# Four column blocks share the opening of a two-block transformer kernel, rows turned beforehand, and sixteen modulation units change place

## The chip, the cores and the metric

The kernel runs on one core of a Trainium2 chip. The metric is the time of one execution on the device in microseconds (us). A core has a matrix engine (TensorE, PE in the rows; its weight loads are PEld), an elementwise engine (VectorE, DVE), an activation engine (ScalarE, ACT), GpSimd (POOL) and SyncE (SP), which here issues the transfers from device memory. Each engine takes its instructions strictly in the order in which they were written for it; semaphores between engines hold an instruction until its inputs are there. SBUF is the on-chip memory with 128 partitions; PSUM has eight banks that matmuls write.

## The reference

256 rows of 1024 features go through two layers of a first block and two of a second. A layer of the first block, cut to what matters here (`cond` is one vector, the same for all rows):

```python
mod = cond @ ada_w[l] + ada_b[l]
sh1, sc1, g1, sh2, sc2, g2, sh3, sc3, g3 = jnp.split(mod, 9, axis=-1)
hn = _modulate(_rms_norm(h, norm_g[l, 0]), sh1, sc1)      # xn * (1 + scale) + shift
h = h + 0.5 * g1 * _swiglu(hn, ffn1_w_in[l], ffn1_w_out[l])
hn = _modulate(_rms_norm(h, norm_g[l, 1]), sh2, sc2)
z = hn @ w_in[l]
# four groups of z: differential attention, convolution, gMLP, forgetting attention
h = h + g2 * (mixed @ w_out[l])
hn = _modulate(_rms_norm(h, norm_g[l, 2]), sh3, sc3)
h = h + 0.5 * g3 * _swiglu(hn, ffn2_w_in[l], ffn2_w_out[l])
```

All of it is float32. `ada_w` is 1024 x 9216 for each layer, so the nine modulation vectors cost 36 MB of weights a layer and next to no matrix work.

## The kernel before

The 256 rows are two row tiles (`tt`), the 1024 features eight feature tiles (`k`) of 128. A float32 product is made from three products of float32r parts: high x high, high x low, low x high. A weight **chunk** is 128 x 1024 numbers, 512 KB: for an input projection two feature tiles by the 512 columns of one column block `b`, so a block has four chunks (`c`); a feed-forward's input has 11 blocks. SyncE loads a chunk (`fetch`, L391 to L401, at most eight outstanding), ScalarE casts it to the high part, and VectorE subtracts that from the chunk to get the low part (`pump`). A stage of one chunk and one row tile is then six matmuls of 128x512.

Modulation comes in **units** of 512 KB, 128 of a vector's 1024 values: VectorE multiplies the unit by the broadcast `cond_row` and sums along the row (`ada_unit`; in the trace CUSTOM_DVE_ANT_0 with `cond_row` among its inputs). Gate vectors (v = 2, 5, 8) go another way, as a running sum with `cond`. Units and chunks lie in one `stream` in the order in which they are loaded and worked on. A table, `among` (L369), spreads the units of the vectors among the chunks of a part: a part is a feed-forward or a mixing of one layer. For the first feed-forward part of layer 0 it names vectors 2, 4, 3, 5 (32 units); for layer 0's mixing vectors 7 and 6 (16 units); the mixing of layer 1 has none.

**The opening.** At the start nothing is there: the first modulation vectors (scale 1, shift 0) and the first weights are loaded together. For c = 0 to 3 the stream holds two feature tiles of scale and shift (four units) and then chunk `c` of the first EARLY = 3 column blocks, so that TensorE can begin with the first two feature tiles. The order of its work is then chunk, row tile, block (`gemm_in`, first lines). The rows are normalized (VectorE, per row), turned by TensorE against an identity into PSUM, four feature tiles to a bank, and ScalarE reads the bank, multiplies by the scale and adds the shift (`ev<-bank,mod,mod`), casts, and VectorE makes the low part (`to_xT`, L695, in four steps of two feature tiles for the first norm). After the opening the other blocks go one after the other, each with all eight feature tiles; a block's result is read from its bank by ScalarE and VectorE (`ev<-bank`, `ev<-ev,bank`), an evacuation.

**What sets the order.** The kernel is written by a Python planner that keeps a clock for each engine (`Plan`, with a cost for each kind of operation). `pump` converts the next chunk or unit when it has landed by the planner's clock and the engines are not too late; `chunk` forces a conversion when TensorE's program needs it; `Background` interleaves the row work and the attention steps. The order that results is fixed at build time. Every recorded operation has the line of the recording helper, L183, so that rows are told apart by their tiles: `c` are buffers of the arena, `bank` PSUM banks, `mod` the modulation vectors, `ev`, `sm`, `st`, `dl` small work tiles, `con` constants.

Of the kernel before, what the change touches and what calls it, by code (L numbers as in the profile page):

```python
# [242 lines left out]
def two_blocks(ctx: ExitStack, tc, w, out, dbg=None, stages=99):  # L243
# [9 lines left out]
    EARLY = 3  # L253
# [115 lines left out]
    among = {0: (modulation(0, 2, 4, 3, 5), 2, 48), 1: (modulation(0, 7, 6), 16, 32), 2: (modulation(0, 8) + modulation(1, 1, 0, 2), 10, 60),  # L369
# [42 lines left out]
    def pump(force=False, most=None, goal=None):  # L412
        while True:
# [7 lines left out]
            if not force and plan.ready(raw) > plan.now + 0.3:  # L421
                return
# [117 lines left out]
    def ada_unit(raw, l, v, kt):  # L540
        key = (l, v)
        if v % 3 != 2:
# [28 lines left out]
    def mod_tile(l, v):  # L571
        if (l, v) not in mod_val:
            mod_val[l, v], mod_there[l, v] = pool.tile([P, KT], F, name=f"mod{l}_{v}"), []
# [21 lines left out]
    class Normed:  # L595
# [3 lines left out]
        def __init__(self, mods=None, gain=None, keep=False, steps=2):  # L599
            self.mods, self.gain, self.keep, self.steps = mods, gain, keep, steps  # L600
# [35 lines left out]
        def chain(self, tt):  # L636
# [9 lines left out]
            by = (lambda pair: all(pair in mod_there.get(m, ()) for m in self.mods), lambda: [mod_val[m] for m in self.mods]) if self.mods else None  # L646
# [4 lines left out]
            yield from to_xT(rows, self.gain, self.xT[tt], by, self.x[tt], there=self.there[tt], have=lambda hf: self.halves[tt] > hf, steps=self.steps)  # L651
# [6 lines left out]
        def finish(self, tt, pair):  # L658
            wait(lambda: len(self.there[tt]) > pair * self.steps // 4, "rows")
# [35 lines left out]
    def to_xT(src, A, dst, mods=None, whole=None, there=None, have=lambda hf: True, steps=2):  # L695
# [14 lines left out]
        def modulated(step):  # L710
            return mods is None or all(mods[0](p) for p in range(4 * step // steps, 4 * (step + 1) // steps))

        yield from turn()
        B = None
        if mods:
            if steps == 2 and not modulated(0):
                yield from turn()
            yield from until(lambda: modulated(0))
            A, B = mods[1]()
        n = KT // steps  # L720
        for step in range(steps):
            hf = step * 2 // steps
            if hf == len(banks):
                yield from turn()
            yield from until(lambda: modulated(step) and (A is None or whole is not None or evr.has(1)))
            a = slice(n * step, n * step + n)
            ps = banks[hf][:, a.start - 4 * hf:a.stop - 4 * hf]
            if A is None:
                split(ps, hi[:, a], lo[:, a])
                psr.put()  # L730
                there.append(step)
                continue
            x = evr.take([P, n, P]) if whole is None else whole[:, a]
            if B is None:
                ve.tensor_tensor(x, ps, A[:, a, None].to_broadcast([P, n, P]), op=OP.mult)
            else:
                for j in range(n):
                    k = n * step + j
                    if steps == 2 and hf:
# [3 lines left out]
            if a.stop == 4 * hf + 4:  # L743
                psr.put()
            split(x, hi[:, a], lo[:, a])
            there.append(step)
            if whole is None:
                evr.put()

# [16 lines left out]
    def gemm_in(n_, blocks, evac):  # L766

        whole, nb = range(4), len(blocks)
        if st["want"] == 0:
            order = [(b, tt, whole[c:c + 1]) for c in whole for tt in range(2) for b in range(EARLY)]  # L770
            order += [(b, tt, whole) for b in range(EARLY, nb) for tt in range(2)]
            mine["quota"] = 4
        else:
            order = [(b, tt, whole) for b in range(nb) for tt in range(2)]
            if len(n_.there[1]) < 2:
# [3 lines left out]
        for b, tt, part in order:  # L779
# [6 lines left out]
            for ci in part:  # L786
# [4 lines left out]
                n_.finish(tt, ci)  # L791
                for k2 in range(2):
                    k = 2 * ci + k2
# [993 lines left out]
```

## Time and profile before

| | |
|---|---|
| median of 3 runs | 1932.78 us (1932.68 to 1933.05) |
| profiled execution, its own time | 1931.21 us |
| its span in the trace | 1929.3 us |
| mean granted clock of TensorE | 0.993 |
| TensorE busy | 1871.3 us, 97% |
| VectorE busy | 1307.2 us, 68% |
| ScalarE busy | 969.6 us, 50% |
| transfers | 397.31 MB, mean 206 GB/s |

TensorE is busy nearly all of the span, and the share of a stage is read from the windows: first the opening (22.6 us, the first float32r matmul, to 58.6), then the rest of layer 0's first feed-forward part (to about 228.6, where the mixing's 128x260 matmuls begin), layer 0's mixing (to 356.4), and layer 1's mixing (745.0 to 848.9). The granted clock of a stretch is in parts of 2.4 GHz; the engine's other level is 1.2 GHz, which a row shows as 0.50.

### The profile page before, as it was taken

How to read it: one execution, taken by the hardware profiler on the slowest of the kernel's cores; microseconds unless marked ns; L12 is line 12 of the kernel's file. 1: busy time of each engine (PE TensorE's matmuls, PEld its weight loads, DVE VectorE, ACT ScalarE, POOL GpSimd, SP SyncE). 2: the span in 40 equal slices, each digit the busy share in tenths (PEclk: the TensorE clock that was granted, in tenths of full speed). 3: DMA queues.
4: the chain of work that ended last, by engine and by line, in shares of the span. 5: the costliest groups of instructions: out<-in, count | busy, mean ns of one | idle time of the engine just before them, and what ended most of it. 6: DMA issues, size and time to landing. Idle time of an engine off the chain costs nothing.

```text
span 1929.3 us, 23834 instructions
## 1 busy us (share of the span) xinstructions
PE 1871.3 (97%) x8672; PEld 1491.6 (77%) x8672; DVE 1307.2 (68%) x2055; ACT 969.6 (50%) x1501; POOL 17.0 (1%) x56
## 2 busy tenths in 40 slices
PE   5999997999999999999999999999999999999998
PEld 3888864688888887658888787888888787888886
DVE  5988598687878876966575646666664646666562
ACT  4544534543544445464454645545553655655451
POOL 0000000000000000000000000000000000000000
PEclk9999998999999999999999999999999999999999
DMA  9988584387868885526574343654574443655460
GB/s 385 335 301 324 177 309 151 108 297 268 320 224 301 291 320 191 184 83 219 176 269 155 121 164 109 201 193 153 163 246 148 142 153 99 199 195 163 144 228 33
DMA packets 110578, 397.31 MB, mean 206 GB/s; under 512 B 12278, under 2 KB 12406, under 8 KB 110460
## 3 DMA queue, kind: packets, MB, share of 16 engines
q1 hardware_dynamic: 109020, 391.88, 58.6%
q10 hardware_dynamic: 1440, 3.91, 0.6%
q8 instruction: 68, 1.11, 0.2%
q14 instruction: 50, 0.41, 0.1%
HBM read 394.69 MB, written 1.05 MB: 205 GB/s over the span
## 4 chain that ended last, share of the span: by engine, by line
PE 85%; DVE 7%; ACT 5%; DMA 2%; issue 1%; POOLq 0%; SPq 0%; POOL 0%; DVEq 0%; ACTq 0%
PE bank L183 85%; DVE c L183 5%; ACT c L183 2%; ACT sm L183 2%; DMA c<-in_ffn_w_in_dram 2%; DVE sm L183 1%; ACT L175 1%; DVE st L183 0%; DMA c<-in_w_out_b_dram 0%; ACT ev L183 0%; DVE ev L183 0%; DMA col<-in_cols_dram 0%; DVE h L183 0%; ACT dl L183 0%; ACT st L183 0%
## 5 line engine op out<-in xcount | busy, mean ns | idle before, releaser
L183 PE MATMUL bank<-c,c 128*128 128x512 f32 (+3 forms) x7392 | 1764.4, 397 | 19.7 <-ACT c L183 15.0
L183 PEld LDWEIGHTS bank<-c,c 128*128 128x128 f32 (+1 forms) x7392 | 1352.2, 189 | 335.7 <-issue 44.7
L183 DVE TENSOR_TENSOR c<-c,c 128x1024 fp32r<-128x1024 f32 (+3 forms) x604 | 709.0, 1197 | 242.6 <-ACT c L183 234.9
L183 ACT CAST c<-c 128x1024 fp32r<-128x1024 f32 (+1 forms) x590 | 588.7, 1036 | 110.3 <-PE bank L183 79.4
L183 ACT ACTIVATE ev<-bank 128x256 f32<-128x256 f32 (+1 forms) x100 | 40.1, 401 | 202.5 <-PE bank L183 202.1
L183 DVE CUSTOM_DVE_ANT_0 c<-c,cond_row,col 128x1024 f32<-128x1024 f32 x96 | 121.9, 1279 | 0.0
L183 ACT CAST c<-bank 128x512 fp32r<-128x512 f32 (+1 forms) x100 | 55.3, 553 | 85.1 <-PE bank L183 85.1
L183 DVE TENSOR_TENSOR c<-bank,c 128x512 fp32r<-128x512 f32 (+2 forms) x108 | 69.9, 649 | 24.4 <-ACT c L183 24.1
L183 DVE TENSOR_TENSOR ev<-ev,bank 128x256 f32<-128x256 f32 x88 | 36.7, 418 | 69.2 <-ACT ev L183 67.8
L183 ACT ACTIVATE ev<-bank,st 128x512 f32<-128x512 f32 x56 | 38.5, 687 | 77.5 <-PE bank L183 77.5
L183 ACT ACTIVATE junk<-h 128x512 f32<-128x512 f32 x44 | 27.7, 631 | 98.2 <-DVE h L183 97.8
L183 PE MATMUL bank<-con,ev 128*128 128x128 f32 x432 | 72.4, 273 | 3.3 <-DVE ev L183 3.3
L183 PEld LDWEIGHTS bank<-con,ev 128*128 128x128 f32 x432 | 55.7, 139 | 25.1 <-issue 3.7
L183 ACT CAST c<-ev 128x512 fp32r<-128x512 f32 (+1 forms) x36 | 20.6, 573 | 91.6 <-DVE ev L183 91.2
L183 ACT ACTIVATE c<-bank,st 128x512 f32<-128x512 f32 x36 | 24.8, 688 | 75.2 <-PE bank L183 69.7
L183 DVE TENSOR_TENSOR ev<-bank,c 128x512 f32<-128x512 f32 x40 | 27.4, 686 | 40.8 <-PE bank L183 40.7
L183 DVE SCALAR_TENSOR_TENSOR c<-c,cond,c 128x1024 f32<-128x1024 f32 x42 | 53.8, 1280 | 0.0
L183 DVE TENSOR_TENSOR ev<-ev 128x512 f32<-128x512 f32 x32 | 22.1, 691 | 45.5 <-ACT ev L183 45.5
L183 DVE SCALAR_TENSOR_TENSOR c<-c,col,c 128x256 f32<-128x256 f32 x120 | 48.8, 479 | 0.0
L183 ACT ACTIVATE sm<-sm,st 128x128 f32<-128x128 f32 x72 | 31.8, 442 | 26.0 <-DVE st L183 26.0
L183 DVE TENSOR_TENSOR c<-ev,c 128x512 fp32r<-128x512 f32 (+1 forms) x36 | 22.8, 633 | 29.8 <-ACT c L183 29.7
L183 DVE TENSOR_TENSOR h<-h,bank 128x512 f32<-128x512 f32 x16 | 10.9, 683 | 42.1 <-PE bank L183 42.1
(104 smaller groups left out, 681.8 us busy)
## 6 DMA issues: line engine op xcount, KB each, us to landing
c<-in_ffn_w_in_dram SPq DMA_DIRECT2D x176, 512.0 KB, 5.7
c<-in_w_in_dram SPq DMA_DIRECT2D x152, 512.0 KB, 4.1
c<-in_ada_w_dram SPq DMA_DIRECT2D x144, 512.0 KB, 5.5
c<-in_ffn_w_out_dram SPq DMA_DIRECT2D x88, 512.0 KB, 5.2
c<-in_w_up_dram SPq DMA_DIRECT2D x64, 512.0 KB, 3.7
c<-in_w_down_dram SPq DMA_DIRECT2D x64, 512.0 KB, 3.8
c<-in_w_out_dram SPq DMA_DIRECT2D x16, 512.0 KB, 6.3
c<-in_w_o_dram SPq DMA_DIRECT2D x16, 512.0 KB, 4.7
```

Source lines behind the costliest of these rows:

```text
L175: self.eng.preload_act_table_set(table)
L183: return fn(*args, **kw)
```

## The change

EARLY goes from 3 to 4, so that four column blocks share the opening, and their eight banks (four blocks, two row tiles) are held at once. The order is chunk, block, row tile. For the first norm, `to_xT` gives way to `first_xT`: all sixteen 128x128 transposes come first and ScalarE copies them from PSUM to an SBUF tile `x`; scaling, cast and split then go from there, in steps that end at 1, 2, 4, 6 and 8 feature tiles (`FIRST`). The matmuls wait for a feature tile, not for a pair. The factor (1 + scale) x g is made once for all eight columns, except for the first norm, where it follows the steps. `pump` holds back unforced conversions until the opening's sixteen chunks are made, and `chunk` forces up to two. In the table `among`, vectors 7 and 6 of layer 0 move from its mixing to its first feed-forward part: 48 units at positions 0 to 50 there, none in the mixing. The main lines:

```diff
-    EARLY = 3
+    EARLY = 4
+    FIRST = [1, 2, 4, 6, 8]
...
-    among = {0: (modulation(0, 2, 4, 3, 5), 2, 48), 1: (modulation(0, 7, 6), 16, 32), 2: (modulation(0, 8) + modulation(1, 1, 0, 2), 10, 60),
+    among = {0: (modulation(0, 2, 4, 3, 5, 7, 6), 0, 50), 2: (modulation(0, 8) + modulation(1, 1, 0, 2), 10, 60),
...
-            if not force and plan.ready(raw) > plan.now + 0.3:
+            if not force and (st["made"] < 4 * EARLY or plan.ready(raw) > plan.now + 0.3):
                 return
...
-            pump(True, goal=i + 1 if i < 4 * EARLY else None)
+            pump(True, goal=min(i + 2, 4 * EARLY) if EARLY <= i < 4 * EARLY else i + 1 if i < EARLY else None)
...
-            if kt % 2:
+            if kt + 1 in (FIRST if key in ((0, 0), (0, 1)) else [KT]):
+                a = slice(mod_there[key], kt + 1)
                 if v % 3 == 1:
-                    a = slice(kt - 1, kt + 1)
-                    ve.scalar_tensor_tensor(t[:, a], t[:, a], 1.0, K("norm_g", 24 * l + 8 * (v // 3) + kt - 1, 2), op0=OP.add, op1=OP.mult)
-                mod_there[key].append(kt // 2)
+                    ve.scalar_tensor_tensor(t[:, a], t[:, a], 1.0, K("norm_g", 24 * l + 8 * (v // 3) + a.start, a.stop - a.start),
+                                            op0=OP.add, op1=OP.mult)
+                mod_there[key] = a.stop
...
+    def first_xT(src, dst, mods, there):
+
+
+        hi, lo = dst
+        yield from until(room)
+        x = arena.take([P, KT, P])
+        for hf in range(2):
+            yield from ripe(src[:, 512 * hf:512 * hf + 512])
+            yield from until(aux_free)
+            ps = aux((P, 4, P))
+            for j in range(4):
+                k = 4 * hf + j
+                pe.transpose(ps[:, j], src[:, P * k:P * k + P], ident)
+            sc_.copy(x[:, 4 * hf:4 * hf + 4], ps)
+            psr.put()
+            there.append(0)
+        for a in (slice(a, b) for a, b in zip([0] + FIRST, FIRST)):
+            made = 0 if a.stop == 1 else 1 if a.stop == 2 else EARLY * (a.start // 2) + 2
+            yield from until(lambda: mods[0](a.stop) and st["made"] >= made)
+            A, B = mods[1]()
+            for k in range(a.start, a.stop):
+                sc_.activation(x[:, k], x[:, k], AF.Identity, scale=A[:, k:k + 1], bias=B[:, k:k + 1])
+            split(x[:, a], hi[:, a], lo[:, a])
+            there.append(a.stop)
+            yield
+        arena.put()
...
-            order = [(b, tt, whole[c:c + 1]) for c in whole for tt in range(2) for b in range(EARLY)]
+            order = [(b, tt, whole[c:c + 1]) for c in whole for b in range(EARLY) for tt in range(2)]
             order += [(b, tt, whole) for b in range(EARLY, nb) for tt in range(2)]
-            mine["quota"] = 4
+            mine["quota"] = 8
...
-                n_.finish(tt, ci)
                 for k2 in range(2):
                     k = 2 * ci + k2
+                    n_.finish(tt, k)
...
-    begin(lambda: all(norms[0].rs[tt] is not None for tt in range(2)))
+    begin(lambda: all(len(norms[0].there[tt]) == 2 for tt in range(2)))
     pump(True, 4)
-    begin(lambda: all(norms[0].there))
+    begin(lambda: all(len(norms[0].there[tt]) == 3 for tt in range(2)))
```

Three places show how the order of instructions moves. The first is VectorE's queue in the second stage of the opening, before: the last modulation unit, the splits of the two row tiles (`c_139`, `c_151`), three low parts of weights (128x1024), and the next stage's first unit.

```order
L183 ISA c_133,mod_0_127<-c_133,cond_row,col 128x1024
L183 ISA mod_0_127 128x1
L183 TENSOR_TENSOR c_139<-ev_221,c_138 128x256
L183 TENSOR_TENSOR c_151<-ev_231,c_150 128x256
L183 TENSOR_TENSOR c_246<-c_136,c_245 128x1024
L183 TENSOR_TENSOR c_259<-c_167,c_258 128x1024
L183 TENSOR_TENSOR c_271<-c_176,c_270 128x1024
L183 ISA c_182,mod_1_123<-c_182,cond_row,col 128x1024
```

The same place of the changed kernel, where the row splits are `c_108` and `c_123`:

```order
L183 ISA c_167,mod_0_158<-c_167,cond_row,col 128x1024
L183 ISA mod_0_158 128x1
L183 TENSOR_TENSOR c_275<-c_180,c_274 128x1024
L183 TENSOR_TENSOR c_281<-c_206,c_280 128x1024
L183 TENSOR_TENSOR c_108<-c_109,c_107 128x256
L183 TENSOR_TENSOR c_123<-c_124,c_122 128x256
L183 TENSOR_TENSOR c_319<-c_226,c_318 128x1024
L183 TENSOR_TENSOR c_325<-c_246,c_324 128x1024
L183 ISA c_262,mod_1_153<-c_262,cond_row,col 128x1024
```

There is one low part of a weight more, and two of the four stand ahead of the row splits. The second place is VectorE's queue at the end of the opening, before: the last row splits, low parts of weights, and between them the evacuations of the opening's banks (`ev_...<-ev_...,bank_...`).

```order
L183 TENSOR_TENSOR c_139<-ev_378,c_138 128x256
L183 TENSOR_TENSOR c_151<-ev_383,c_150 128x256
L183 TENSOR_TENSOR c_401<-c_305,c_400 128x1024
L183 TENSOR_TENSOR c_416<-c_327,c_415 128x1024
L183 TENSOR_TENSOR c_425<-c_342,c_424 128x1024
L183 TENSOR_TENSOR c_431<-c_351,c_430 128x1024
L183 TENSOR_TENSOR ev_440<-ev_439,bank_162 128x256
L183 TENSOR_TENSOR c_447<-c_354,c_446 128x1024
L183 TENSOR_TENSOR ev_456<-ev_455,bank_190 128x256
```

The same place of the changed kernel. Here `c_554` and `c_560` are the low parts of the opening's chunks 14 and 15, which are the last chunks of column blocks 2 and 3; the banks 175, 194, 201 and 214 belong to blocks 0 and 1.

```order
L183 TENSOR_TENSOR ev_516<-ev_515,bank_175 128x256
L183 TENSOR_TENSOR ev_527<-ev_526,bank_194 128x256
L183 TENSOR_TENSOR ev_537<-ev_536,bank_201 128x256
L183 TENSOR_TENSOR ev_550<-ev_549,bank_214 128x256
L183 TENSOR_TENSOR c_554<-c_415,c_553 128x1024
L183 TENSOR_TENSOR c_560<-c_421,c_559 128x1024
L183 TENSOR_TENSOR c_569<-c_448,c_568 128x1024
```

Before, all of the opening's low parts stand ahead of the first evacuation; now two stand behind four evacuations. The third place is VectorE's queue within layer 0's mixing, before: units of vector 7 (`mod_7_2137`), the finishing operation of a pair, and products of the convolution (`c_2141`).

```order
L183 TENSOR_TENSOR c_2284<-c_2108,c_2283 128x1024
L183 ISA c_2110,mod_7_2137<-c_2110,cond_row,col 128x1024
L183 ISA mod_7_2137 128x1
L183 SCALAR_TENSOR_TENSOR mod_7_2137<-mod_7_2137,col 128x2
L183 ISA c_2139,mod_7_2137<-c_2139,cond_row,col 128x1024
L183 ISA mod_7_2137 128x1
L183 ISA c_2207,mod_7_2137<-c_2207,cond_row,col 128x1024
L183 ISA mod_7_2137 128x1
L183 SCALAR_TENSOR_TENSOR mod_7_2137<-mod_7_2137,col 128x2
L183 ISA c_2248,mod_7_2137<-c_2248,cond_row,col 128x1024
```

The same place of the changed kernel (`c_2167` is the convolution there):

```order
L183 TENSOR_TENSOR c_2222<-c_2001,c_2221 128x1024
L183 SCALAR_TENSOR_TENSOR c_2167<-c_2040,col,c_2167 128x256 x8
L183 TENSOR_TENSOR dl_2203<-bank_2160,st_2242 128x8x64
L183 TENSOR_REDUCE st_2257<-ev_2256 128x8
L183 TENSOR_TENSOR c_2264<-c_2092,c_2263 128x1024
L183 SCALAR_TENSOR_TENSOR c_2167<-c_2040,col,c_2167 128x256 x8
```

The units are gone from between the weights' low parts, the convolution and the attention's steps.

## Rows read from the trace of the kernel before

**Rows 1.** Windows by stage: stretch, length, busy (instructions), granted clock, DMA share, GB/s.

```profile
22.60:58.60 36.00, 32.35 (x117) 24.97 (x117) 29.24 (x44) 17.12 (x29) 0.00 (x0) 0.91 1.03 409
58.60:208.70 150.10, 150.07 (x679) 123.03 (x680) 125.29 (x164) 74.74 (x100) 0.00 (x0) 1.00 0.83 295
...
228.60:356.40 127.80, 109.34 (x455) 70.97 (x453) 103.97 (x268) 62.24 (x144) 0.97 (x5) 0.93 0.54 194
...
745.00:848.90 103.90, 100.19 (x456) 65.82 (x454) 83.61 (x231) 62.18 (x145) 0.97 (x5) 1.00 0.47 160
```

**Rows 2.** Timeline, VectorE, first stage: start, busy, operation, [idle before, releaser].

```profile
14.47 1.28 DVE L183 CUSTOM_DVE_ANT_0 c<-c,cond_row,col 128x1024 f32<-128x1024 f32 x1
...
19.49 0.08 DVE L183 DVE_READ_ACCUMULATOR2_ANT mod<- 128x1 f32 x1
20.54 0.43 DVE L183 TENSOR_TENSOR c<-ev,c 128x256 fp32r<-128x256 f32 x1 [0.96 <-ACT c L183]
21.68 0.43 DVE L183 TENSOR_TENSOR c<-ev,c 128x256 fp32r<-128x256 f32 x1 [0.72 <-ACT c L183]
22.63 3.50 DVE L183 TENSOR_TENSOR c<-c,c 128x1024 fp32r<-128x1024 f32 x3 [0.52 <-ACT c L183]
26.04 1.28 DVE L183 CUSTOM_DVE_ANT_0 c<-c,cond_row,col 128x1024 f32<-128x1024 f32 x1
```

**Rows 3.** Timeline, TensorE, the opening.

```profile
22.65 0.80 PE L183 MATMUL bank<-c,c 128*128 128x512 f32 x1 [6.92 <-ACT c L183]
23.91 7.94 PE L183 MATMUL bank<-c,c 128*128 128x512 f32 x23 [0.46 <-DVE c L183]
...
32.48 11.25 PE L183 MATMUL bank<-c,c 128*128 128x512 f32 x48
45.80 0.49 PE L183 MATMUL bank<-c,c 128*128 128x512 f32 x1 [2.07 <-ACT c L183]
47.05 11.23 PE L183 MATMUL bank<-c,c 128*128 128x512 f32 x36 [0.76 <-DVE c L183]
58.63 3.70 PE L183 MATMUL bank<-c,c 128*128 128x512 f32 x15 [0.34 <-DVE c L183]
```

**Rows 4.** Windows, TensorE alone: stretch, length, busy, granted clock, DMA share, GB/s.

```profile
46.00:54.00 8.00, 7.24 (x19) 0.57 1.03 409
760.00:768.00 8.00, 5.75 (x24) 1.00 0.23 91
```

**Rows 5.** Windows of the instructions on `cond_row`: length, VectorE, ScalarE, clock, DMA.

```profile
60.00:208.70 148.70, 20.45 (x16) 0.00 (x0) 1.00 0.83 294
228.60:356.40 127.80, 20.14 (x16) 0.00 (x0) 0.93 0.54 194
745.00:848.90 103.90, 0.00 (x0) 0.00 (x0) 1.00 0.47 160
```

**Rows 6.** Windows, all engines, the stretch of layer 0's mixing that holds its units.

```profile
248.90:304.00 55.10, 47.61 (x198) 34.41 (x197) 54.62 (x132) 17.89 (x45) 0.00 (x0) 0.93 0.81 300
```

**Rows 7.** Timeline, TensorE, layer 0's mixing.

```profile
301.62 1.65 PE L183 MATMUL bank<-c 32*128 32x256 f32 x6 [7.49 <-DVE c L183]
```

**Rows 8.** Groups by line and shape, 0 to 230: count, busy us, mean ns, idle before.

```profile
L183 DVE TENSOR_TENSOR c<-c,c 128x1024 fp32r<-128x1024 f32 x72 | 86.1, 1221 | 10.3 <-ACT c L183 9.1 <-issue 1.1
L183 ACT CAST c<-c 128x1024 fp32r<-128x1024 f32 x72 | 72.0, 1048 | 14.9 <-PE bank L183 14.8
...
L183 ACT ACTIVATE ev<-bank 128x256 f32<-128x256 f32 x22 | 8.5, 385 | 34.8 <-PE bank L183 34.6
...
L183 ACT ACTIVATE ev<-bank,mod,mod 128x128 f32<-128x128 f32 x16 | 6.9, 454 | 25.4 <-DVE mod L183 25.4
...
L183 ACT CAST ones_r<-con 128x128 fp32r<-128x128 f32 x1 | 0.3, 290 | 0.0
```

**Rows 9.** Waits, 58.6 to 208.7: who waits for whom, us in total, times, longest.

```profile
DVE ev L183 <- ACT ev L183: 7.0, 5, 1.7
DVE c L183 <- ACT c L183: 7.0, 10, 2.6
```

More of the change, by code (lines that the diff above doesn't have):

```diff
@@ L650, in chain @@
                 self.x[tt] = arena.take([P, KT, P])
-            yield from to_xT(rows, self.gain, self.xT[tt], by, self.x[tt], there=self.there[tt], have=lambda hf: self.halves[tt] > hf, steps=self.steps)
+            if self.first:
+                yield from first_xT(rows, self.xT[tt], by, self.there[tt])
+            else:
+                yield from to_xT(rows, self.gain, self.xT[tt], by, self.x[tt], there=self.there[tt], have=lambda hf: self.halves[tt] > hf)
             if self.mods:
@@ L656, in chain, with finish @@
             st["hurry"] -= 1
-        def finish(self, tt, pair):
-            wait(lambda: len(self.there[tt]) > pair * self.steps // 4, "rows")
+        def finish(self, tt, k):
+            wait(lambda: self.there[tt] and self.there[tt][-1] > k, "rows")
         def free(self):
@@ L693, in start, with to_xT @@
                 (nc.sync, nc.scalar)[hf].dma_start(out[tt * P:tt * P + P, s], h[tt][:, s])
-    def to_xT(src, A, dst, mods=None, whole=None, there=None, have=lambda hf: True, steps=2):
+    def to_xT(src, A, dst, mods=None, whole=None, there=None, have=lambda hf: True):
         hi, lo = dst
@@ L715, in to_xT @@
         if mods:
-            if steps == 2 and not modulated(0):
+            if not mods[0](KT):
                 yield from turn()
-            yield from until(lambda: modulated(0))
+            yield from until(lambda: mods[0](KT))
             A, B = mods[1]()
-        n = KT // steps
-        for step in range(steps):
-            hf = step * 2 // steps
+        for hf in range(2):
             if hf == len(banks):
                 yield from turn()
-            yield from until(lambda: modulated(step) and (A is None or whole is not None or evr.has(1)))
-            a = slice(n * step, n * step + n)
-            ps = banks[hf][:, a.start - 4 * hf:a.stop - 4 * hf]
+            yield from until(lambda: A is None or whole is not None or evr.has(1))
+            a, ps = slice(4 * hf, 4 * hf + 4), banks[hf]
             if A is None:
@@ L730, in to_xT @@
                 psr.put()
[L731 removed]
+                there.append(a.stop)
                 continue
[L733 removed]
+            x = evr.take([P, 4, P]) if whole is None else whole[:, a]
             if B is None:
[L735 removed]
+                ve.tensor_tensor(x, ps, A[:, a, None].to_broadcast([P, 4, P]), op=OP.mult)
             else:
[L737 to L739 removed]
+                for j in range(4):
+                    k = 4 * hf + j
+                    if hf:
                         ve.tensor_scalar(x[:, j], ps[:, j], A[:, k:k + 1], B[:, k:k + 1], op0=OP.mult, op1=OP.add)
@@ L1614, in two_blocks @@
         for i in range(3):
-            norms.append(Normed(mods=((l, 3 * i + 1), (l, 3 * i)), keep=i == 1, steps=2 if norms else 4))
+            norms.append(Normed(mods=((l, 3 * i + 1), (l, 3 * i)), keep=i == 1, first=not norms))
     for l in range(L):
```

21 lines of the change are left out of this document (11 added, 10 removed).

## The prediction

> **What bounds the kernel now.** I read the windows by stage first, then one engine's rows inside the stages that the edit touches. In [rows 1] TensorE is busy for 150.07 of 150.10 us in the rest of the first feed-forward part (58.6 to 208.7): there only TensorE's own work counts, and VectorE's 125.29 us and the transfers (share 0.83) are cover. Two stretches are different. In the opening, 22.6 to 58.6, TensorE has 32.35 of 36.00 at a granted clock of 0.91. In layer 0's mixing, 228.6 to 356.4, it has 109.34 of 127.80 at 0.93. Layer 1's mixing, the same computation without modulation units [rows 5], takes 103.90 with 100.19 busy at 1.00. So the two mixing parts differ by 23.9 us: TensorE idles 18.46 us in one and 3.71 in the other, which is 14.75, and the other 9.15 is time in which its work went slower.
>
> What holds the opening is a turn-taking of VectorE and ScalarE, seen in [rows 2]. VectorE reduces four modulation units (14.47 to 19.57), waits 0.96 for ScalarE's cast of the first row tile, splits it, waits 0.72 for the second, then 0.52 for the cast of a weight chunk, then makes three low parts (3.50); only then come the next four units, at 26.04. The period is 11.57 us, 2.20 of it waiting. TensorE gets 36 matmuls in a period; 48 of them took 11.25 [rows 3], so it needs 8.44 and runs dry: it stood still before 45.80 (2.07) and before the 47.05 row (0.76), and in the 8 us from 46 on its granted clock was 0.57 [rows 4], the lower of its two levels (1.2 and 2.4 GHz) for most of it, a loss of 0.43 x 8 = 3.4 us.
>
> What holds layer 0's mixing is VectorE between 248.9 and 304.0: 54.62 of 55.10 us busy [rows 6]. All 16 units lie in that stretch, 20.14 us [rows 5]. TensorE's 7.49 idle us there are one stop before 301.62, released by VectorE [rows 7]; the later stops in this part follow from that delay.
>
> **The opening.** After the change the row tiles are turned first: 16 transposes and four ScalarE copies that fall before 18 us. They cost nothing, because ScalarE's first modulation work waits for VectorE's first units anyway (two of the four are done at 17.0; the second row tile is ready at 14.5, and its two copies of 128x512, each at most two of the 128x256 reads at 0.39, take 1.5 behind the transposes [rows 2, 8]). TensorE's start then follows from the rows. First feature tile: two units end at 14.47 + 5.10/2 = 17.0; ScalarE scales and casts two tiles of 128x128, 2 x (0.45 + 0.29), and casts the first chunk, 1.05 [rows 8]: 19.6, against 22.65 before. The second matmul waits for the low part: four units end at 19.57, two small splits (0.29 each, estimated from the cast of the same shape) and a subtraction (3.50/3 = 1.17) give 21.3 plus two semaphore steps, 21.5, against 23.91.
>
> Then stages of four column blocks. VectorE per stage: four units 5.10, four subtractions 4.67, two row splits 0.86, together 10.6. ScalarE: four casts of 1.05, four scalings of 0.45, two casts at most as long as the splits, 6.9. Transfers: eight units of 524 KB at 409 GB/s [rows 1], 10.25. TensorE: 48 matmuls, 11.25. TensorE is the longest, provided that VectorE no longer waits its 2.20; the first order shows why it need not: two weight subtractions now stand between the units and the row splits, two behind them. The first 23 matmuls took 7.94 where 23 x 0.2344 = 5.39, a slow start of 2.55, which I keep. Stage 0 ends at 21.5 + 47 x 0.2344 + 2.55 = 35.1, stage 1 at 46.3, and the 110th matmul starts 13 later, at 49.4. Before it started at 58.63 [rows 3]. **Term 1: -9.2 us**; if VectorE keeps its waits the period is 12.8, 1.55 a stage for three stages, and the term is -4.5. I take -9.2, since the rows behind each wait have been moved.
>
> The Trainium skill speaks against this: "DMA: Bandwidth & Descriptors", Specifications, gives a limit of about 358 GB/s from device memory to one core, by which a stage of eight units would take 11.7 us, above TensorE's 11.25, and four stages about 1.9 us more, for a predicted time of 1910.1. The row shows 409 GB/s over 36 us; the measurement decides.
>
> **A new stop at its end.** The second order shows what the edit does behind the last stage: the subtractions of chunks 14 and 15 (inputs c_415, c_421) now stand behind the evacuations of four banks, and ScalarE's casts do likewise. The last evacuation's bank is finished only when TensorE has done column block 1's second row tile, and by then TensorE needs chunk 14. So it stands for one ScalarE activation (0.39), one cast (1.05) and one subtraction (1.22, slightly more than one of three in a row): 2.66 [rows 8]. That a half clock follows is seen behind the stop of 2.83 at 46 (3.4 lost) and not in 760 to 768, where TensorE stood for 2.25 of the 8 us and the clock stayed 1.00 [rows 4]; bounds 0 and 3.4, and I take 2.0, since the new stop's length is nearer to the first. **Term 2: +4.7**, between 2.7 and 6.1.
>
> On the clock the Trainium skill ("TensorE: Matmul & The Clock Gate", What's actually happening) says that the low level is the default and that activity lifts it, so that every stop can cost it again; by that alone the stop would be 6.1 and the time 1909.6. The row of 760 to 768 shows a pause that did not.
>
> **Sixteen units into the first feed-forward part.** They cost VectorE 20.45/16 = 1.28 each there [rows 5], 20.4. VectorE's idle time in that stretch is 150.10 - 125.29 = 24.8, so it would be at 145.7 of 150.1; the transfers would be 44.3 + 8.4 MB at 409 GB/s, 129 us. Cover is there, but thin: if it fails, the price is rival B's. SyncE issues these loads in the order of the stream, up to eight ahead, so a unit that waits for VectorE delays the weight loads behind it; weight casts and subtractions queue behind units on VectorE in the same way. **Term 3: 0**, bounds 0 and 9.3; a gain is excluded, since TensorE had 0.03 us idle there.
>
> **Layer 0's mixing.** Without its units VectorE has 34.5 us of work in a stretch of 55.1, and SyncE 16 fewer loads. The third order shows products of the attention and weight subtractions following one another directly. The nearest row above is layer 1: -23.9. The nearest below is the one stop in the full stretch: -7.5. I take the 20.1 us that leave a VectorE that is full; what is late next is TensorE itself, busy 100.19 of 103.90 in layer 1 [rows 1]. **Term 4: -20.1.**
>
> The finishing of a modulation vector in one operation for eight columns in place of four, and the waits by feature tile in place of pairs, take away a few operations on 128x2 pieces, under a busy TensorE: nothing.
>
> **Sum.** -9.2 + 4.7 + 0 - 20.1 = -24.6 on the profiled execution's 1931.21: 1906.6. That execution lies 1.57 under the median of 1932.78, so the median comes to 1908.2.
>
> **Rivals.**
> **B, VectorE becomes the bound of the first feed-forward part.** Its waits for ScalarE there were 7.0 and 7.0 us [rows 9]. If they remain, it needs 125.3 + 20.1 + 14.0 = 159.4 against 150.1: +9.3, a time of 1917.5. For it: the stretch before had cover of only 24.8 us. Against: it waits for ScalarE where its queue holds nothing else that is ready, and sixteen more units are such work. The transfers would do the same if they were slower than their row: from 22.6 on this stretch and the opening move 14.7 + 44.3 + 8.4 = 67.4 MB [rows 1], which at 409 GB/s are there at 187.4, 17 us before the stretch ends at 204.2. By the 358 GB/s of the Trainium skill ("DMA: Bandwidth & Descriptors", Specifications) they would be there at 210.8, 6.6 late, for a time of 1914.8; the row of [rows 1] with 409 speaks against it.
> **C, mixing gives back only its one stop.** The remaining idle and slow time is layer 0's own order: -7.5 for -20.1, and 1920.8. Against it speaks that layer 1 has neither.
> **D, no new stop and the whole difference of the layers:** -9.2 - 23.9 = -33.1, a time of 1899.7. It needs the casts of chunks 14 and 15 to be done earlier than their place in the queue allows.
> **E, slower.** The stop of term 2 comes back at each of the seven later column blocks of this part, since each one's subtractions can land behind the evacuation of the block before, with VectorE now 97% full: 7 x 4.7 = 32.9, which gives +8.3 and 1941.1. It decides from the sixth stop on. Against: TensorE ran through this stretch with the same queues, and only the opening holds four blocks open at once.
> **F, it does not do what it says.** VectorE keeps its turn-taking (-4.5), the stop takes that back (+4.7), and the 20.1 us come back as TensorE's waits in the stretch that takes the units: 1933.
>
> **How the numbers follow.** Forecast 0.57, B 0.18, C 0.12, D 0.06, E 0.04, F 0.03. The forecast's own bounds: best -9.2 + 2.7 - 23.9 = -30.4 (1902.4), worst of its terms -4.5 + 6.1 - 20.1 = -18.5 (1914.3). To hold 8 in 10 the range goes from D to C, 1899 to 1921; E and F stay out. Measurement can tell about 0.2%, 3.9 us, from no change: faster 0.93, same 0.03, slower 0.04.
>
> **What would show it.** First matmul at 19.6, 110th matmul at about 49.4, VectorE waiting under 1 us a stage; one stop of about 2.7 us near 63, with or without clock 0.5 behind it; the first 128x260 matmul at about 224 in place of 228.6, with TensorE over 149 busy in any 150 before it; mixing 104 to 110 us long. Wrong would be a stage period near 12.8, several stops between 66 and 205, or a mixing part that still idles 10 us.

## The result, and the profile after

The changed kernel takes 1906.26 us (median of 4 runs, 1904.18 to 1907.24) against 1932.91 for the kernel before beside it (4 runs, 1932.68 to 1934.27). The ratio is 0.9859, with a 95% interval of 0.9842 to 0.9876. The prediction was 1908.2 in a range of 1899 to 1921, faster with a chance of 0.93. The profiled execution of the changed kernel took 1907.24 us, with a span of 1905.5: 23.8 us less span than before.

Windows by stage of the changed kernel answer to [rows 1] (stretch, length; busy and instructions of TensorE, weight loads, VectorE, ScalarE and GpSimd; granted clock, DMA share, GB/s):

```profile
19.70:60.90 41.20, 40.36 (x168) 32.89 (x169) 37.28 (x74) 26.46 (x44) 0.00 (x0) 1.00 1.03 410
60.90:70.50 9.60, 7.11 (x34) 5.17 (x31) 8.19 (x10) 6.74 (x10) 0.00 (x0) 1.00 1.03 410
70.50:202.00 131.50, 130.65 (x589) 106.77 (x590) 127.25 (x160) 61.45 (x79) 0.00 (x0) 1.00 0.95 361
...
222.00:330.30 108.30, 103.64 (x452) 67.47 (x450) 84.05 (x233) 60.22 (x143) 0.74 (x2) 0.97 0.45 151
...
720.00:825.00 105.00, 101.25 (x451) 66.45 (x451) 82.97 (x229) 61.05 (x142) 0.74 (x2) 0.98 0.46 156
```

The opening is full: 40.36 of 41.20 us of TensorE, where it had 32.35 of 36.00. VectorE has 127.25 of 131.50 in the feed-forward part and TensorE still 130.65. Layer 0's mixing is 108.3 us long, not 127.8, and close to layer 1's.

The timeline of VectorE in the second stage, which answers to [rows 2] (start, busy, operation, [idle before, releaser]):

```profile
25.72 1.28 DVE L183 CUSTOM_DVE_ANT_0 c<-c,cond_row,col 128x1024 f32<-128x1024 f32 x1
...
30.74 3.03 DVE L183 TENSOR_TENSOR c<-c,c 128x1024 fp32r<-128x1024 f32 x4
33.99 2.36 DVE L183 TENSOR_TENSOR c<-c,c 128x1024 fp32r<-128x1024 f32 x2 [0.23 <-ACT c L183]
36.27 1.28 DVE L183 CUSTOM_DVE_ANT_0 c<-c,cond_row,col 128x1024 f32<-128x1024 f32 x1
```

The period is 36.27 - 25.72 = 10.55 us with four column blocks, and of the 2.20 us of waiting 0.23 is left. The row of four is two weight subtractions and two row splits without a wait between them.

TensorE's timeline up to the mixing answers to [rows 3] (only rows behind an idle time are shown):

```profile
19.78 0.80 PE L183 MATMUL bank<-c,c 128*128 128x512 f32 x1 [3.22 <-ACT c L183]
21.34 39.79 PE L183 MATMUL bank<-c,c 128*128 128x512 f32 x167 [0.76 <-DVE c L183]
...
62.75 0.49 PE L183 MATMUL bank<-c,c 128*128 128x512 f32 x1 [1.41 <-ACT c L183]
64.01 0.73 PE L183 MATMUL bank<-c,c 128*128 128x512 f32 x2 [0.77 <-DVE c L183]
...
70.81 0.44 PE L183 MATMUL bank<-con,ev 128*128 128x128 f32 x2 [0.63 <-DVE ev L183]
...
99.45 0.73 PE L183 MATMUL bank<-c,c 128*128 128x512 f32 x2 [0.55 <-DVE c L183]
```

From 21.34 on, 167 matmuls follow one another; then come the new stop (1.41 and 0.77) and two small ones.

Four points in the program, and its end, show where the time went (start of the operation in us; the last column is the difference).

| | before | after | |
|---|---|---|---|
| 110th float32r matmul of the opening | 58.63 | 47.59 | -11.04 |
| first row of 128x260 matmuls (the mixing begins) | 228.62 | 222.07 | -6.55 |
| last transposes of layer 0's mixing | 356.46 | 330.36 | -26.10 |
| last transposes of layer 1's mixing | 848.89 | 824.35 | -24.54 |
| end of the span | 1929.3 | 1905.5 | -23.8 |

(In the changed kernel three of the 128x260 matmuls, 0.12 us each, stand ahead of that row, so that the second line is 0.35 us short of the real difference, and the mixing's 108.3 is 0.35 us short of a like length.) Counted alike, the opening gives 11.0, the stops behind it take 4.1 back, the mixing gives 19.2, and 2.3 are lost where nothing was changed.

### The profile page after: what moved, and what is told of

The parts are those of the page before. It is cut to its first block, busy times and chain, and to the rows that moved or that the text cites. A ratio compares the mean times of both kernels' runs of the same rounds, so it can differ in the third digit from the quotient of the medians.

```text
span 1905.5 us, 23848 instructions
## 1 busy us (share of the span) xinstructions
PE 1864.3 (98%) x8672; PEld 1487.9 (78%) x8672; DVE 1303.6 (68%) x2044; ACT 972.5 (51%) x1506; POOL 17.0 (1%) x56
## 4 chain that ended last, share of the span: by engine, by line
PE 87%; DVE 5%; ACT 5%; issue 1%; DMA 1%; POOL 0%; ACTq 0%; POOLq 0%; DVEq 0%
PE bank L183 87%; DVE c L183 3%; ACT sm L183 2%; ACT c L183 2%; DVE sm L183 1%; ACT L175 1%; DMA cond_row<-in_c_dram 0%; DVE ev L183 0%; DMA c<-in_ada_w_dram 0%; DMA c<-in_w_out_b_dram 0%; DVE st L183 0%; DVE h L183 0%; ACT ev L183 0%; ACT junk L183 0%; ACT dl L183 0%
## 5 line engine op out<-in xcount | busy, mean ns | idle before, releaser
L183 DVE TENSOR_TENSOR c<-c,c 128x1024 fp32r<-128x1024 f32 (+4 forms) x614 | 711.5, 1182 | 233.4 <-ACT c L183 225.4
L183 ACT CAST c<-c 128x1024 fp32r<-128x1024 f32 (+4 forms) x600 | 592.0, 1025 | 112.7 <-PE bank L183 74.7
L183 ACT CAST c<-ev 128x512 fp32r<-128x512 f32 x28 | 17.4, 620 | 91.4 <-DVE ev L183 91.2
L183 DVE TENSOR_TENSOR c<-ev,c 128x512 fp32r<-128x512 f32 x28 | 19.4, 692 | 23.1 <-ACT c L183 23.0
```

What stands on the lines that cost most here:

```text
L183: return fn(*args, **kw)
```

## The experiments

The theory: the opening gains because VectorE no longer takes turns with ScalarE; the mixing gains because VectorE was full there; in the feed-forward part the units are covered. Rival B held that VectorE becomes the bound there. Each ratio below is against runs of the kernel before made beside that experiment. Their medians were 1931.14 to 1931.42 us, 1.5 to 1.8 below the 1932.91 of the result, so that a difference of a few us between an experiment and the changed kernel's 1906.26 is partly this one.

**The units alone.** The kernel before with one line of the table (the units spread over positions 0 to 54, where the changed kernel has 0 to 50):

```diff
-    among = {0: (modulation(0, 2, 4, 3, 5), 2, 48), 1: (modulation(0, 7, 6), 16, 32), 2: (modulation(0, 8) + modulation(1, 1, 0, 2), 10, 60),
+    among = {0: (modulation(0, 2, 4, 3, 5, 7, 6), 0, 54), 2: (modulation(0, 8) + modulation(1, 1, 0, 2), 10, 60),
```

> The kernel before with one line changed: vectors 7 and 6 of layer 0 move from its mixing to the first feed-forward part (positions 0 to 54 there); the opening keeps three blocks. My theory (the units cost layer 0's mixing 20 us because VectorE is full there, and are covered in the feed-forward part): the mixing takes 108 us in place of 127.8, the first 128x260 matmul stays within 2 us of 228.6, the time is 1912 to 1915. Rival B (VectorE becomes the bound where the units go): the 128x260 matmul comes 5 to 9 us later and the time is 1918 to 1922.

1917.25 us, ratio 0.9926 (0.9909 to 0.9942), above my 1912 to 1915 and just below the rival's range. The mixing did what the theory said, 106.3 us long (234.46 to 340.80). The 128x260 matmuls came at 234.46, 5.8 us later than before, as rival B had it. TensorE's timeline had two idle rows there, and ScalarE's shows what stood before them:

```profile
74.69 0.49 PE L183 MATMUL bank<-c,c 128*128 128x512 f32 x1 [2.68 <-ACT c L183]
75.95 0.73 PE L183 MATMUL bank<-c,c 128*128 128x512 f32 x2 [0.76 <-DVE c L183]
```

```profile
66.07 1.28 ACT L175 ACT_TABLE_LOAD   x1
69.42 0.20 ACT L183 ACTIVATE st<-st 128x2 f32<-128x2 f32 x1 [2.07 <-DVE st L183]
70.86 0.20 ACT L183 ACTIVATE st<-st 128x2 f32<-128x2 f32 x1 [1.23 <-DVE st L183]
...
71.27 1.28 ACT L175 ACT_TABLE_LOAD   x1
72.56 0.66 ACT L183 ACTIVATE ev<-bank 128x256 f32<-128x256 f32 x2
73.11 0.59 ACT L183 CAST c<-bank 128x512 fp32r<-128x512 f32 x1
73.57 2.96 ACT L183 CAST c<-c 128x1024 fp32r<-128x1024 f32 x3
```

From 66.07 to 72.55 ScalarE did little but the per-layer preparation: two table loads and two tiny activations that waited for VectorE. The casts of weights stood behind it. From 76 to 80 the granted clock was 0.57, another 1.7 us. So the delay could be the preparation's place, not VectorE's load; the next run parts the two.

**The units alone, with the preparation put off.** Besides the line above:

```diff
     def layer_setup(l):
+        yield from until(lambda: plan.now > 120.0)
```

> The kernel before with the sixteen units moved and, besides, the small per-layer preparation (gains, two table loads on ScalarE) put off until 120 us of the planner's clock. In the run that moved the units alone, the first 128x260 matmul came at 234.5 in place of 228.6, with one stop of 2.68 and 0.76 us at 74.7 behind that preparation, and half the clock behind it. My theory (the preparation's new place made that stop, VectorE's load did not): no stop near 75, the 128x260 matmul at 228 to 230, the time 1910 to 1913. Rival B (VectorE is the bound where the units go): stops elsewhere between 60 and 200, the 128x260 matmul still at 233 or later, 1916 or more.

1912.82 us, ratio 0.9902 (0.9887 to 0.9916), and the 128x260 matmuls at 228.86, 0.24 from where they were before. The window of the rest of the feed-forward part (columns as above):

```profile
58.60:208.70 150.10, 150.10 (x680) 122.94 (x681) 144.16 (x201) 74.85 (x100) 0.00 (x0) 1.00 0.93 351
```

VectorE has 144.16 of 150.10 us, 18.9 more than in [rows 1], and TensorE has no idle time at all. Rival B falls: the cover holds at 96%, with this spread of the units.

**The opening alone.** The changed kernel with the old table:

```diff
-    among = {0: (modulation(0, 2, 4, 3, 5, 7, 6), 0, 50), 2: (modulation(0, 8) + modulation(1, 1, 0, 2), 10, 60),
+    among = {0: (modulation(0, 2, 4, 3, 5), 2, 48), 1: (modulation(0, 7, 6), 16, 32), 2: (modulation(0, 8) + modulation(1, 1, 0, 2), 10, 60),
```

> The changed kernel with the old table: vectors 7 and 6 stay in layer 0's mixing, the opening is the new one. My theory (the two edits add up): the first 128x260 matmul at 221 to 222.5, the mixing again 126 to 129 us long, the time 1925 to 1927. Rival (the opening's gain is given back later when VectorE's load stays in the mixing, or the mixing was already part of the opening's gain): the time is 1930 or more, or 1915 or less.

1922.85 us, ratio 0.9956 (0.9942 to 0.9971): 2.15 us below my range, between my case and the rival's. The 128x260 matmuls came at 222.75, 0.25 past my range, and the mixing kept its stop:

```profile
222.70:351.80 129.10, 110.80 (x455) 71.43 (x453) 103.52 (x265) 62.42 (x144) 0.97 (x5) 0.91 0.53 192
```

```profile
295.30 1.65 PE L183 MATMUL bank<-c 32*128 32x256 f32 x6 [6.91 <-DVE c L183]
```

129.1 us, against 127.8 in [rows 1] and 108.3 with the units gone. The profiled execution of this kernel took 1926.42 us and lay above its other three (1921.94 to 1923.66), so this one profile shows the marks, and not where the others were 3 to 4 us shorter. The two edits add up: 0.44% for the opening and 0.98% for the units (with the preparation out of the way) make 1.42%, and both together measured 1.41%. Each of the three is known to some 0.15%, and the run for the units has the wider spread and the later preparation, so the sum agrees within that and no closer.

**Half of the units.** The changed kernel, with vector 6 back in the mixing:

```diff
-    among = {0: (modulation(0, 2, 4, 3, 5, 7, 6), 0, 50), 2: (modulation(0, 8) + modulation(1, 1, 0, 2), 10, 60),
+    among = {0: (modulation(0, 2, 4, 3, 5, 7), 0, 50), 1: (modulation(0, 6), 16, 32), 2: (modulation(0, 8) + modulation(1, 1, 0, 2), 10, 60),
```

> The changed kernel with only vector 7 moved: eight units go back into layer 0's mixing. My theory (VectorE is full in that stretch and each unit costs its own 1.28 us): the mixing takes 106 + 10 = 114 to 119 us, the time 1911 to 1916. Rival (a threshold: eight units still fit under TensorE's work, or one unit too many already brings the whole stop): the mixing 109 us or less, or 124 or more.

1914.50 us, ratio 0.9911 (0.9897 to 0.9926). The mixing's window:

```profile
221.30:339.40 118.10, 107.85 (x455) 70.16 (x453) 93.23 (x247) 64.83 (x147) 0.97 (x5) 0.94 0.50 175
```

118.1 us: near the middle between 108.3 and 129.1. Eight units cost about 10 us in the mixing, their own 10.08 us of VectorE's time, and no threshold shows at eight. (Part of it is TensorE's idle time and part its clock, 0.94 here against 0.97 and 0.91.) The units bring loads as well as work for VectorE, and no run parts the two; it is [rows 6], with VectorE at 54.62 of 55.10 us and a DMA share of 0.81, that speaks for VectorE.

**The units left out altogether.** The changed kernel, with the third norm of layer 0 reading other vectors, so that its result is another one:

```diff
-    among = {0: (modulation(0, 2, 4, 3, 5, 7, 6), 0, 50), 2: (modulation(0, 8) + modulation(1, 1, 0, 2), 10, 60),
+    among = {0: (modulation(0, 2, 4, 3, 5), 0, 50), 2: (modulation(0, 8) + modulation(1, 1, 0, 2), 10, 60),
...
-            norms.append(Normed(mods=((l, 3 * i + 1), (l, 3 * i)), keep=i == 1, first=not norms))
+            norms.append(Normed(mods=((0, 4), (0, 3)) if (l, i) == (0, 2) else ((l, 3 * i + 1), (l, 3 * i)), keep=i == 1, first=not norms))
```

> The changed kernel with the sixteen units left out: the third norm of layer 0 uses vectors 4 and 3 in place of 7 and 6, which are not computed at all. It shows what the units cost where they were put. My theory (covered): the 128x260 matmul comes at most 1.5 us before 222.07 and the time is 1904 to 1906. Rival B (VectorE is the bound there): it comes 5 us earlier or more and the time is under 1901.

1902.14 us (ratio 0.9846, 0.9831 to 0.9861), 1.86 below what I gave as its lower end, but the 128x260 matmuls came at 221.43, 0.64 before the changed kernel's, as I expected of the cover. The start of the opening was slower here (110th matmul at 48.24, not 47.59). From that matmul on it is 173.19 us against 174.48, and 0.35 of the difference are the three 128x260 matmuls ahead of the mark: where the units were put they cost about 0.9 us. The rest lies behind the mark: the mixing took 105.5 us, in another order than the changed kernel's (the first 24 of the 128x260 matmuls in one row), and layer 1's 103.9 (715.38 to 819.28) against 105.4 (718.92 to 824.35). The difference in layer 1 is the clock's and is taken up below.

**The last two chunks of the opening.** The changed kernel, with the conversions of chunks 14 and 15 written as soon as the last row split is there:

```diff
                     k = 2 * ci + k2
                     n_.finish(tt, k)
+                    if st["want"] < 4 * EARLY and (b, tt, k) == (0, 1, KT - 1):
+                        pump(True, goal=4 * EARLY)
```

> The changed kernel with one addition: the casts and subtractions of the opening's chunks 14 and 15 are written when the last row split is there, so that on VectorE and ScalarE they stand behind one evacuation and not behind four. My theory (the 2.2 us stop at 62.75 and 64.01 is the wait for these two behind the evacuations): both rows are gone, the 128x260 matmul comes 1.5 to 2.5 us earlier than 222.07, the time is 1903.5 to 1905. Rival (the stop only passes to the next block, whose weights now queue behind the delayed evacuations): a new idle row of 1 us or more before 75 us and a time of 1906 or more.

1902.88 us (1902.68 to 1902.94), ratio 0.9849 (0.9835 to 0.9864). That is 3.4 us under the changed kernel, of which 1.8 is the difference between the two sets of runs of the kernel before; the interval overlaps the changed kernel's, 0.9842 to 0.9876. So the times alone do not show the gain; the marks in the trace do. All of TensorE's idle rows of more than 0.4 us between the opening and the mixing:

```profile
68.42 0.44 PE L183 MATMUL bank<-con,ev 128*128 128x128 f32 x2 [0.66 <-DVE ev L183]
...
97.65 0.73 PE L183 MATMUL bank<-c,c 128*128 128x512 f32 x2 [1.15 <-DVE c L183]
```

The two rows at 62.75 and 64.01 are gone, and the 128x260 matmuls come at 220.28, 1.8 us earlier (1.5 counted from the 110th matmul). The stop was the wait for these two chunks behind four evacuations. The mixing of this profile is shorter too, by 1.9 us: a row of four matmuls that took 3.78 us at half the clock in the changed kernel took 1.98 here.

```profile
307.54 3.78 PE L183 MATMUL bank<-c,c 128*128 128x512 f32 x4 [0.68 <-ACT c L183]
```

```profile
304.86 1.98 PE L183 MATMUL bank<-c,c 128*128 128x512 f32 x4 [0.68 <-ACT c L183]
```

The first of these rows is the changed kernel's. A second measurement of the version with early last chunks is below.

**Three blocks with turned rows.** The changed kernel with EARLY = 3, six banks held, the row work allowed one chunk earlier, and the units at positions 0 to 54:

```diff
-    EARLY = 4
+    EARLY = 3
...
-    among = {0: (modulation(0, 2, 4, 3, 5, 7, 6), 0, 50), 2: (modulation(0, 8) + modulation(1, 1, 0, 2), 10, 60),
+    among = {0: (modulation(0, 2, 4, 3, 5, 7, 6), 0, 54), 2: (modulation(0, 8) + modulation(1, 1, 0, 2), 10, 60),
...
-            made = 0 if a.stop == 1 else 1 if a.stop == 2 else EARLY * (a.start // 2) + 2
+            made = 0 if a.stop == 1 else 1 if a.stop == 2 else EARLY * (a.start // 2) + 1
...
-            mine["quota"] = 8
+            mine["quota"] = 6
```

> The changed kernel with three column blocks in the opening in place of four (and a step of the row work allowed one chunk earlier, without which the order can't be built). It parts turning the rows beforehand from the fourth block. By the sum of VectorE's work a stage takes 9.6 us there (four units 5.0, three subtractions 3.5, splits 0.85, a short wait) against TensorE's 8.2, so TensorE waits again in each stage: the 110th matmul at 51 to 53 (58.6 before, 47.5 with four blocks), so that turning the rows brings about 6.5 us of the 11 and the fourth block the rest. Rival 1 (turning the rows does nothing by itself): 57 or later. Rival 2 (the fourth block does nothing): 49 or earlier.

TensorE's timeline:

```profile
21.44 10.11 PE L183 MATMUL bank<-c,c 128*128 128x512 f32 x37 [0.76 <-DVE c L183]
32.45 16.71 PE L183 MATMUL bank<-c,c 128*128 128x512 f32 x70 [0.90 <-DVE c L183]
50.77 0.74 PE L183 MATMUL bank<-c,c 128*128 128x512 f32 x2 [1.61 <-ACT c L183]
...
66.48 0.80 PE L183 MATMUL bank<-c,c 128*128 128x512 f32 x1 [5.46 <-ACT c L183]
```

With the one matmul before them, 1 + 37 + 70 = 108 come before the row at 50.77, and the 110th starts at 51.11: in these two profiles 7.5 us of the 11 come with the rows turned beforehand, the other 3.5 with the fourth block. TensorE waits at the start of two of the three later stages (32.45 and 50.77); the sum had it wait at each. The whole time, 1914.67 us (ratio 0.9910, 0.9895 to 0.9925), tells less, since in this order there is a stop of 5.46 us before 66.48: from 60.43 to 65.09 ScalarE is at the preparation, with the casts of weights behind it.

**Row tile outside.** The changed kernel with the old nesting of the opening's matmuls:

```diff
-            order = [(b, tt, whole[c:c + 1]) for c in whole for b in range(EARLY) for tt in range(2)]
+            order = [(b, tt, whole[c:c + 1]) for c in whole for tt in range(2) for b in range(EARLY)]
```

> The changed kernel with the old nesting of the opening's matmuls: row tile outside, block inside. My theory (the nesting is not what took the waits away): TensorE runs through the opening as before, the 110th matmul at 47 to 49, a stop of 1.5 to 3 us near 60, the time 1905 to 1908. Rival (four chunks are needed within half a stage, so that TensorE waits for VectorE at the start of each): idle rows of 0.5 us or more at each stage and the 110th matmul at 50 or later, 1909 or more.

1904.60 us (1904.45 to 1904.78), ratio 0.9860 (0.9844 to 0.9877), with the 128x260 matmuls at 221.99 (222.07). The stop is there too, 1.41 and 0.77 us at 60.56 and 61.82. The time is 0.4 us under my range, and the 110th matmul at 48.34 within it. The nesting shows no effect.

**A wider spread of the units,** on top of the early last chunks:

```diff
-    among = {0: (modulation(0, 2, 4, 3, 5, 7, 6), 0, 50), 2: (modulation(0, 8) + modulation(1, 1, 0, 2), 10, 60),
+    among = {0: (modulation(0, 2, 4, 3, 5, 7, 6), 0, 54), 2: (modulation(0, 8) + modulation(1, 1, 0, 2), 10, 60),
```

> The version with the opening's last two chunks converted early, and the 48 units spread over positions 0 to 54 of the feed-forward part in place of 0 to 50 (0.89 units to a chunk, not 0.96). In that version one stop of 1.15 us is left at 97.65, released by VectorE, which is busy without a gap from 87 to 101. My theory (units too dense for VectorE there): the stop at 97 shrinks to under 0.5 us, the 128x260 matmul comes 0.7 to 1.5 us before 220.3, the time is 1901 to 1902.5. Rival (the stop belongs to the gate vector's last step, which waits on its own chain): it stays at 1.0 to 1.3 us and the time at 1902.5 to 1903.5.

> The version with the last two chunks converted early, unchanged, beside the wider spread on the same chip, so that a difference of 1 us can be told. It also shows whether the clock behind the same pause of 1.52 and 0.76 us in layer 1's mixing (733.1) falls to the lower level again: if the level follows from the kernel alone, the 17 matmuls behind it take 5.7 us as in that version's first profile; if it is chance, they may take 4.2.

1900.99 us (1900.17 to 1902.32), ratio 0.9839 (0.9822 to 0.9855), against 1902.07 (1901.13 to 1903.07), 0.9842 (0.9827 to 0.9857), for the narrower spread beside it. The stop at 97 is gone, as I expected of units that are too dense there, but the 128x260 matmuls come at 223.46, 3.2 us after the 220.28 that they were to beat, since a new stop stands before the mixing:

```profile
218.22 0.49 PE L183 MATMUL bank<-c,c 128*128 128x512 f32 x1 [1.84 <-ACT c L183]
219.90 0.78 PE L183 MATMUL bank<-c,c 128*128 128x512 f32 x2 [1.18 <-DVE c L183]
```

The mixing behind it has another order (the first 24 of the 128x260 matmuls in one row) and takes 102.1 us, 4.2 less than with the narrower spread. The 1 us between the two is not clear of their scatter. That either beats the changed kernel is likely, but the times do not show it: its 0.9859 comes from other runs, and its interval, 0.9842 to 0.9876, overlaps both.

## Why the prediction was right

**Term 1, the opening: -9.2 predicted, -11.0 measured.** The steps held: first matmul at 19.6 (19.78), second at 21.5 (21.34), VectorE's period 10.6 (10.55), TensorE the longest. The term was too small by 1.8 us, mostly in two sizes. I took 0.2344 us for a matmul from 48 in 11.25 us, but a row's length counts the whole of its last matmul: a row of the changed kernel at 169.03 has 174 in 39.83 us, at most 0.2289 each, 0.6 us less over 108. And I kept a slow start of 2.55 us as if it were fixed. It is the lower clock at the start, and it varies (last section); with 0.2289 this profile has 39.79 - 167 x 0.2289 = 1.6. Over the eight profiles that have this opening the 110th matmul starts between 47.29 and 48.88, so the term lies between -9.75 and -11.34, and the changed kernel's own profile is one of the quick ones. The transfers kept up, at 410 GB/s over 41 us: no wait of TensorE in the opening has a transfer as its releaser. The 358 GB/s that the Trainium skill gives ("DMA: Bandwidth & Descriptors", Specifications) did not bind here; the measured 410 decides.

**Term 2, the new stop: +4.7 predicted.** The place and the cause were right, as the run with early last chunks shows. The idle time was 1.41 + 0.77 = 2.18, not 2.66. The chain itself had the predicted length, as these rows show, with those at 62.75 and 64.01 above:

```profile
60.97 0.38 PE L183 MATMUL bank<-con,ev 128*128 128x128 f32 x2
61.38 0.38 ACT L183 ACTIVATE ev<-bank 128x256 f32<-128x256 f32 x1 [1.20 <-PE bank L183]
61.66 3.89 ACT L183 CAST c<-c 128x1024 fp32r<-128x1024 f32 x4
62.73 3.50 DVE L183 TENSOR_TENSOR c<-c,c 128x1024 fp32r<-128x1024 f32 x3 [0.51 <-ACT c L183]
```

TensorE runs out at 61.35, and activation, cast and subtraction take until 64.01, which is 2.66. But one matmul (62.75, 0.49 us) needs only the cast, and ran while VectorE subtracted. The sum had TensorE stand for the whole chain. Half the clock did not follow: TensorE's windows of the changed kernel (length, busy, clock, DMA share, GB/s) have 1.00.

```profile
62.00:64.00 2.00, 0.49 (x1) 1.00 1.03 410
64.00:66.00 2.00, 1.99 (x12) 1.00 1.03 410
```

In the run with the opening alone the same stop (1.41 and 0.76) was followed by half a clock, 0.72 on average from 64 to 70, a loss of 1.7 us. So the term was 2.2 in one profile, below its lower bound of 2.7, and 3.9 in another, and 4.7 was high.

**Term 3, the sixteen units in the feed-forward part: 0 predicted.** Two small stops, 0.63 and 0.55, are in the timeline; without the units the first is still there (0.61 before 71.45) and the second is gone. The price was about 0.9 us. The mark at the mixing's start was predicted at 224 and came at 222.07, mostly for terms 1 and 2.

**Term 4, the mixing: -20.1 predicted, -19.55 measured** (-19.2 counted alike). Here the step was to take VectorE's own time of the units as the gain, and the run with half of them bears it out: about 10 us for eight. The changed kernel's mixing was unlucky by the 1.8 us at 307.54; the run with the units alone had 106.3, and in the order of the wider spread it is 102.1.

**What was not in the sum.** From layer 0's mixing to the end, 2.3 us were lost in code that the change does not touch: 1.57 in layer 1's mixing (105.43 against 103.86), which is the clock's doing (last section), and 0.74 in the 1080 us behind it, whose cause I did not find. The medians moved by 26.65, 2.7 more than the two profiled executions; where, no profile shows.

**How near the sum came is partly luck.** It was -24.6, and the two spans differ by -23.8. Term 1 was 1.8 too small and terms 2 and 3 together 0.6 too dear (4.7 for 4.1); against them stand 0.9 too much in term 4 and the 2.3 that no term had. The errors cancel to 0.8. The cause in each of the four places was the predicted one all the same, as the runs above bear out.

**The rivals.** B fell with the preparation put off; what looked like B in the first run was the preparation, with its table loads, in front of weight casts. C fell: the mixing gave back 19.2 us and not 7.5. D was too good for this kernel. The version with early last chunks and the wider spread comes near it: 1900.99, which is 30.4 us under the kernel before beside it, against the 33.1 of D. E did not come: behind the opening only 0.63 and 0.55 us are left. F did not come.

## What to carry over

Where the elementwise engine is full, work that can be done elsewhere costs its own time there and little in a stage whose matrix work hides it (here about 20 us against 0.9); look for the full stretch (54.62 of 55.10 in [rows 6]), not for the engine's share of the whole span. Two engines that take turns lose both engines' waits; put work of the next step between request and answer in the in-order queue, and the waits go without any work being saved. When an edit moves the order, look for what newly stands in front of the next weights: here a handful of evacuations cost 2.2 us, and two tiny activations with two table loads cost 3.4 and then 1.7 by the clock.

## What the runs showed of the hardware

**The slow start is the clock's and varies.** The kernel with the early last chunks was profiled twice. The row of 167 matmuls behind the first took 39.57 us in one profile and 41.03 in the other, with no wait inside it in either. The second's windows of TensorE show the lower level:

```profile
20.00:24.00 4.00, 2.94 (x7) 0.59 1.03 410
24.00:28.00 4.00, 4.00 (x12) 0.56 1.03 410
28.00:32.00 4.00, 4.00 (x19) 1.00 1.03 410
```

In the kernel before, the same stretch has 10 matmuls from 24 to 28, slower than these, with a clock of 1.00 in the record:

```profile
24.00:28.00 4.00, 4.00 (x10) 1.00 1.03 410
```

In both stretches a matmul starts 0.43 us after the one before it, and 0.23 us once the slow part is over; the clock record of that profile of the kernel before has its first entry at 29.15. So at the start of an execution the recorded clock can be missing, and the pace of the matmuls tells more. In the old opening this costs nothing that shows: 5 to 12 slow matmuls leave the 110th at 58.50 to 58.63 in its three profiles (the kernel before and the two runs with the units alone), because TensorE has to wait later all the same. In the new one, where TensorE does not wait, 7 to 14 of them move it from 47.29 to 48.88.

**The same pause, two outcomes.** In layer 1's mixing every profile has a pause of about 1.5 and 0.76 us before 17 matmuls. They took 5.73 us in the changed kernel, 4.16 in the version with the wider spread and 4.13 in the kernel before (in this order):

```profile
736.89 0.50 PE L183 MATMUL bank<-c,c 128*128 128x512 f32 x1 [1.52 <-ACT c L183]
738.15 5.73 PE L183 MATMUL bank<-c,c 128*128 128x512 f32 x17 [0.76 <-DVE c L183]
```

```profile
732.09 0.50 PE L183 MATMUL bank<-c,c 128*128 128x512 f32 x1 [1.52 <-ACT c L183]
733.35 4.16 PE L183 MATMUL bank<-c,c 128*128 128x512 f32 x17 [0.76 <-DVE c L183]
```

```profile
764.27 4.13 PE L183 MATMUL bank<-c,c 128*128 128x512 f32 x17 [0.75 <-DVE c L183]
```

Over the twelve profiles of this case seven paid (5.5 to 5.8 us) and five did not (4.1 to 4.2). In the seven the recorded clock falls to 0.50 at the pause; in the five it stays at 1.00. The kernel that was profiled twice paid both times, and the seven are just those whose mixing of layer 0, 500 us earlier, has three of the 128x260 matmuls ahead of its row, so it may not be mere chance. But in the 380 us ahead of the pause TensorE, VectorE and ScalarE have the same rows in the same order in the changed kernel and in the version with the wider spread, and what decides stays open. It is worth 1.6 us in this place alone, as much as some of the terms above.
